# One encoder layer on one core: mixed tokens stored by token tile, pinned splits of the paired projections, and conditioning, combination and gate sums moved to other steps

## The chip, the cores and the metric

The kernel runs on one core of one Trainium2 chip. Time is device microseconds of one execution; the time before is the median of three runs. A profiled execution has a time of its own and a span, which runs from the first to the last recorded instruction. The engines are named as the profile names them: PE (TensorE, with PEld for its weight loads), DVE (VectorE), ACT (ScalarE), POOL (GpSimd) and SP (SyncE, which here only issues DMAs).

## The reference

One layer of an encoder for 1024 tokens of width 1024, float32 throughout:

```
mod = silu(c) @ w_ada + b_ada                      # sh1, sc1, gt1, sh2, sc2, gt2
h = rms_norm(x, g1) * (1 + sc1) + sh1
qa, ka, va, qb, kb, vb, gates = split(h @ w_in)
o_a = neighbourhood_attention(rms_norm(qa), rms_norm(ka), va, rpb)       # 8 heads on a 16 x 64 grid
for g, (window, dilation) in enumerate(((128, 1), (512, 4), (2048, 16))): # 4 heads each, partial rotary
    outs[g], lses[g] = dilated_window_attention(qb, kb, vb, window, dilation)
o_b = sum_g softmax_g(lses)[g] * outs[g]
merged = sigmoid(gate_a) * (o_a @ w_proj_a) + sigmoid(gate_b) * (o_b @ w_proj_b)
x = x + gt1 * (merged @ w_o)
h2 = rms_norm(x, g2) * (1 + sc2) + sh2
x = x + gt2 * ((silu(a) * up) @ w_ffn_out),  a, up = split(h2 @ w_ffn_in)
```

## The kernel before, in words

**Precision.** Every large product is made of three matrix multiplications. An operand is split into a high part (`whi`, ACT, a copy into the type fp32r) and a low part (`wlo`, the operand minus its high part, on DVE or POOL); `wsplit` does this. PE then adds high by high, high by low and low by high in PSUM (`PASS`).

**Fewer products.** Some of the large products are made by a seven-product scheme for 2 x 2 blocks: sums and differences of the operands' blocks are formed, seven block products replace eight. The token side of these sums ("mixed tokens") is made once, by `t_piece` in steps 9 to 26, and is written in high and low parts to the DRAM tensor `t_d`. There are four mixed blocks, named by `TD`: x1, w22, x3, x2, each 512 tokens (four tiles of 128) by 512 features (four slices of 128).

**The middle part of the kernel** is a loop over steps n = 6 to 91. In each step PE gets a few chunks of projection work from a list, `stream`, and one round of attention of an earlier unit (scores, transposes, product with v). Units are column groups of the projection: units 1 to 3 one at a time, units 4 to 9 as three pairs (`pair_units`). A pair has the products p1, p2, x1, x2, x4, x3, w22, each of four token tiles by four chunks. For a product, `when(s - 28 + 4*k, load)` loads weight slice k, `mix` forms the weight sum on POOL (tile `chain` or in place in `raw`), and `split` makes its high and low parts; `sload` loads one token tile of the mixed tokens (`smix`, high and low) from `t_d`. Pairs begin at about steps 28, 44 and 60; from step 58 on (`PAIRED`) attention runs in every step.

**What else is in these steps.** `ada_step` works on the conditioning: 64 small steps, each one multiply-add on DVE over a 128 x 512 piece of `w_ada` (tile `wa`, acc at L328 and L330), with one 512 KB load for two steps. `w1_combos` forms sums of the feed-forward weights on POOL for two column groups and writes them to `w1_d` (`w1m` loads, L881 to L887, stores at L889). `combine_prep` and `combine_step` combine the three dilated groups, in twelve pieces: DVE spreads the softmax weights over a tile `fb` (L720), PE transposes it (L729), DVE multiplies with the attention output `ut` that has been loaded from `u_d`, and adds into `oacc` (L737, L739, L740). From step 74 on `gate_prep` prepares the gate weights of column pairs (sums at L794, L796, L801, then `wsplit`), and from step 76 on `gate_pre` puts their products into the steps (L806), which read the tokens in `hT` as moving operand. For the phase "x1" that operand is the mixed block, reloaded from `t_d` into `hT` by `mixed_load`.

**What sets the order.** PE's instructions run in the order of the program. On ACT, DVE, POOL and SP a planner orders instructions by priority and readiness; those handed to `pin` keep the order of the program among themselves. Each engine then works through its queue strictly in order: an instruction that waits holds what is queued behind it, and a DMA that waits on SP holds all later loads. Tiles come from rings of buffers: `big` has 8, `raw` 6, the rings `hi` and `lo` 10 each.

Of the kernel before, what the change touches and what calls it, by code (L numbers as in the profile page):

```python
# [10 lines left out]
F32 = mybir.dt.float32  # L11
# [12 lines left out]
NRAW, NHL = 6, 10  # L24
# [5 lines left out]
GPHASE = ("w11", "w12", "x1", "x4")  # L30
GPREP = {74: (0, 0), 77: (0, 1), 82: (1, 0), 84: (1, 1), 86: (2, 0), 88: (2, 1), 90: (3, 0)}
GLOAD = {81: 1, 85: 2, 89: 3}
W1MIX = 36
MC11 = {0: (5, 6, 7, 2), 1: (0, 1)}
MKEEP = {3: 3, 4: 4, 5: 5, 6: 6, 7: 7}
MSLOT = {4: 2, 5: 0, 6: 1}
# [2 lines left out]
PP, QT, AQ, AT, AV = 100, 0, 0, 0, 0  # L39
EDGE, CFILL, AFILL, OFILL = 480, 64, 384, 32  # L40
WARM = 40
PAIRED, RBT, COMB = 58, 7, 68
XSQ = "avavaaaa"
XSC = "ddddvvvv"
XE = ("av", "vv", "aa", "aa", "vv", "aa", "va", "va")
# [3 lines left out]
def hybrid_layer(ctx: ExitStack, tc: tile.TileContext, x, colp, wada1, wada2, bada2, wqkv, wg, wpa, wpb,  # L49
# [17 lines left out]
    v_d = tc.dram_tile([8, S, 128], F32, name="v_d")  # L67
    sig_d = tc.dram_tile([KT, 5, 128, 512], F32, name="sig_d")
    h_d = tc.dram_tile([8, 128, S], F32, name="h_d")
    t_d = tc.dram_tile([2, 4, 128, 4, 512], F32, name="t_d")  # L70
    ga_d = tc.dram_tile([7, HT, 128, 512], F32, name="ga_d")
    x2_d = tc.dram_tile([S, D], F32, name="x2_d")
    w1_d = tc.dram_tile([2, 4, 128, 512], F32, name="w1_d")
# [41 lines left out]
    def fview(ap):  # L115
        return ap.bitcast(F32)
# [5 lines left out]
            tc.keep_in_program_order(d)  # L122
        return raw[:, :n]

    def wsplit(r, eng=None):
        n = r.shape[1]
        hi = wp.tile([128, 512], F32R, tag="hi", bufs=NHL, name="whi")
        lo = wp.tile([128, 512], F32R, tag="lo", bufs=NHL, name="wlo")
        nc.scalar.activation(hi[:, :n], r, AF.Copy)  # L129
        (eng or nc.gpsimd).tensor_sub(lo[:, :n], r, fview(hi[:, :n]))  # L130
        return hi, lo

# [568 lines left out]
    def combine_prep(i):  # L701
        pr, g, hf = i // 6, (i % 6) // 2, i % 2
        if g == 0 and hf == 0:
            cb["acc"] = big("oacc")
        ut = wp.tile([128, 512], F32, tag="raw", bufs=NRAW, name="ut")
        u = u_d[g * 2 + pr]
        if g == 0:
            pin(nc.sync.dma_start(ut, u[:, hf * 512:hf * 512 + 512]))
            uv = ut
        elif g == 1:  # L710
            pin(nc.sync.dma_start(ut.rearrange("p (r i) -> p r i", r=4),
                                  u.rearrange("p (r h i) -> p h r i", r=4, h=2)[:, hf]))
            uv = ut.rearrange("p (r i) -> p i r", r=4)
        else:
            pin(nc.sync.dma_start(ut.rearrange("p (t i) -> p t i", t=8),
                                  u.rearrange("p (t i) -> p t i", t=8)[:, :, hf * 64:hf * 64 + 64]))
            uv = ut.rearrange("p (t i) -> p i t", t=8)
        fb = ap_.tile([128, 4, 2, 64], F32, tag=("bm", "rtab")[i % 2], bufs=1, name="fb")
        for hd in range(2):
            nc.vector.tensor_copy(fb[:, :, hd, :], cb["fe"][:, g, hf * 4:hf * 4 + 4, pr, hd, None]  # L720
                                  .to_broadcast([128, 4, 64]))
        cb[i] = (fb, ut, uv, cb["acc"])
# [37 lines left out]

    def mixed_load(nm):
        for q in range(2):
            pin(nc.sync.dma_start(fview(hblk(*TBLK[nm])[q]), t_d[q, TD[nm]]))

    def gate_raw(i, q):
        return wload(wg[i, :, 4 * q:4 * q + 4, :], 512, True)
# [8 lines left out]
    def gate_prep(p, part):  # L775
        pr = GPAIRS[p]
        if part == 0:
            for i in pr if p == 0 else ():
                for q in (0, 1):
                    graw[i, q] = gate_raw(i, q)  # L780
            for nm, q in (("w11", 0), ("w12", 1)):
                for i in pr:
                    gwt[i, nm] = wsplit(graw[i, q])
            return
        if p == 0:
            z = big("wgx")
            for i in pr:
                for q in (2, 3):
                    graw[i, q] = gate_raw(i, q) if i == pr[0] else z[:, 512 * q - 1024:512 * q - 512]
            for q in (2, 3):  # L790
                pin(nc.sync.dma_start(graw[pr[1], q], wg[pr[1], :, 4 * q:4 * q + 4, :]))
        for i in pr:
            r = [graw.pop((i, q)) for q in range(4)]
            nc.vector.tensor_add(r[2], r[2], r[3])  # L794
            gwt[i, "x1"] = wsplit(r[2])
            nc.vector.tensor_sub(r[2], r[2], r[0])  # L796
            if p < 3:
                nc.sync.dma_start(sig_d[i, 4], r[2])
            else:
                glate[i] = r[2], r[3]  # L800
            nc.vector.tensor_sub(r[1], r[1], r[2])  # L801
            gwt[i, "x4"] = wsplit(r[1], nc.vector)

    def gate_mm(pb, w, b, k):
        for q, (x, y) in enumerate(PASS):
# [10 lines left out]
    def gate_pre(n):  # L816

        p, ph = divmod(n, 4)
        nm = GPHASE[ph]

        def chunk(c):
            j, k = divmod(c, 4)
            i = GPAIRS[p][j]
            if k == 0:
                gbank[i] = bank("d")
            gate_mm(gbank[i], gwt[i, nm], hblk(*TBLK[nm]), k)
            if k < 3:
                return
            if ph == 0:
                gacc[i] = [None, ap_.tile([128, 512], F32, tag=("bm", "rtab")[j], bufs=1, name="ga")]  # L830
            elif j == 0:
                z = big("gc")
                for jj in range(2):
                    g = gacc[GPAIRS[p][jj]]
                    g[len(g) if ph > 1 else 0:len(g) + 1 if ph > 1 else 1] = [z[:, 512 * jj:512 * jj + 512]]
            if ph == 0:
                nc.scalar.activation(gacc[i][1], gbank[i], AF.Copy)  # L837
            else:
                gate_open_out(i, nm, gbank[i])
            m = (1, 0, 2, 3)[ph]  # L840
            nc.sync.dma_start(sig_d[i, m], gacc[i][m])

        return [lambda c=c: chunk(c) for c in range(8)]
# [4 lines left out]
    def t_piece(m, part):  # L848
# [15 lines left out]
        else:  # L864
            for a in (0, 2):
                pin(nc.vector.tensor_sub(lo[:, a:a + 2], y[:, a:a + 2], fview(hi[:, a:a + 2])))
            for q, z in enumerate((hi, lo)):
                pin(nc.sync.dma_start(t_d[q, :, :, kk, 256 * pc:256 * pc + 256].rearrange("s p c -> p s c"), fview(z)))

    w1c = {}  # L870

# [226 lines left out]
    def pair_units(ua):  # L1098
        ub = ua + 1
        chain, ch = [], {}  # L1100
        for nm in PROD:
# [3 lines left out]
            for k in range(4):  # L1105
# [16 lines left out]
                        pin(nc.gpsimd.tensor_sub(ch[k], r[k], ch[k]))  # L1122

                def split(k=k, nm=nm, r=r, w=w):
                    w[k] = wsplit(ch[k] if nm in ("x1", "x2", "x3") else r[k], nc.vector if k % 2 else None)

                when(s - 28 + 4 * k, load)
                when(s - 12 + 2 * k, mix)
# [1 line left out]
            for t in range(4):  # L1130
                sm = {}
                if nm in TD:
                    def sload(t=t, nm=nm, sm=sm):
                        for q, tag in enumerate(("hi", "lo")):
                            z = wp.tile([128, 512], F32R, tag=tag, bufs=NHL, name="smix")
                            pin(nc.sync.dma_start(fview(z).rearrange("p (k q) -> p k q", k=4),
                                                  t_d[q, TD[nm], :, :, 128 * t:128 * t + 128]))
                            sm[q] = z

                    when(s + 4 * t - 10, sload)  # L1140
# [33 lines left out]
    for n in range(6, 92):  # L1174
# [82 lines left out]
                    at_turn(I, 1)  # L1257
        while chunks:
            chunk()
        for _ in range(0 if n < 8 else 2 if 28 <= n < PAIRED and n % 2 == 0 else 1):  # L1260
            if ada_state["i"] < 67:
                ada_step()
        for m in range(8):
# [4 lines left out]
                hT[q][0, 1] = quarter(q, 0, 1)  # L1268
            mixed_load("x1")
        for j in range(2):  # L1270
            if 0 <= n - W1MIX - 4 * j < 5:
                w1_combos(j, n - W1MIX - 4 * j)
        if n in GPREP:
            gate_prep(*GPREP[n])
        if n in GLOAD:
# [11 lines left out]
        elif 6 <= u < 10 and t == RBT:  # L1287
            bias_tabs(units[u])

    fill(ap_, AFILL, "afill")  # L1290

    ap_.release()
# [29 lines left out]
    def gate_prod(i, nm):  # L1322
        p = gate_bank()
        for k in range(4):
            gate_mm(p, gwt[i, nm], hblk(*TBLK[nm]), k)
        return p

    def room(n, shape, name, dtype=F32):
# [598 lines left out]
```

## Time and profile before

| | us |
|---|---|
| median of 3 runs | 1535.08 (1532.36 to 1535.8) |
| profiled execution, its own time | 1534.09 |
| its span | 1532.3 |
| PE busy | 1470.1 |
| DVE busy | 1118.4 |
| ACT busy | 715.4 |
| POOL busy | 668.0 |
| mean granted TensorE clock | 0.983 |

Read it by stages. Up to about 200 us the kernel loads, normalises and projects units 0 to 3; from about 200 to 540 us it works on the three pairs; from about 540 to 640 us come the last attention steps and the first gate products; after that the rest of the gates, the merge, the output projection and the feed-forward part. A row of a timeline gives start, duration, engine, line, operation and tiles; what stands in square brackets is the idle time of the engine just before it and what ended that idle time. The granted clock (PEclk) is a share of TensorE's full speed.

### The profile page before, as it was taken

How to read it: one execution, taken by the hardware profiler on the slowest of the kernel's cores; microseconds unless marked ns; L12 is line 12 of the kernel's file. 1: busy time of each engine (PE TensorE's matmuls, PEld its weight loads, DVE VectorE, ACT ScalarE, POOL GpSimd, SP SyncE). 2: the span in 40 equal slices, each digit the busy share in tenths (PEclk: the TensorE clock that was granted, in tenths of full speed). 3: DMA queues.
4: the chain of work that ended last, by engine and by line, in shares of the span. 5: the costliest groups of instructions: out<-in, count | busy, mean ns of one | idle time of the engine just before them, and what ended most of it. 6: DMA issues, size and time to landing. Idle time of an engine off the chain costs nothing. (4 is left out here: it accounts for less than half of the span.)

```text
span 1532.3 us, 24444 instructions
## 1 busy us (share of the span) xinstructions
PE 1470.1 (96%) x8024; PEld 1246.5 (81%) x8024; DVE 1118.4 (73%) x2210; ACT 715.4 (47%) x1807; POOL 668.0 (44%) x640
## 2 busy tenths in 40 slices
PE   8999989779899889999999999999999999999998
PEld 7999978668788767788888888888888888887886
DVE  6787767857888965468584488778867777599468
ACT  5657654544677756446442254222323233343442
POOL 0454344664133102345451120577777776104464
PEclk9999999888999999999999999999999999999999
DMA  9646577679656665494444135345433334798352
GB/s 365 239 156 224 173 247 240 203 246 306 197 169 205 182 192 209 155 359 143 129 135 168 69 110 165 112 157 164 166 132 107 107 104 146 259 375 278 98 153 101
DMA packets 211439, 285.16 MB, mean 186 GB/s; under 512 B 29136, under 2 KB 128112, under 8 KB 209520
## 3 DMA queue, kind: packets, MB, share of 16 engines
q1 hardware_dynamic: 192736, 269.96, 53.3%
q10 hardware_dynamic: 18576, 13.64, 2.7%
q8 instruction: 64, 1.05, 0.3%
q14 instruction: 63, 0.52, 0.1%
HBM read 218.67 MB, written 64.86 MB: 185 GB/s over the span
## 5 line engine op out<-in xcount | busy, mean ns | idle before, releaser
L129 ACT ACTIVATE whi<-raw 128x512 fp32r<-128x512 f32 (+2 forms) x313 | 182.6, 594 | 224.1 <-PE ps_t L1762 33.9
L130 POOL TENSOR_TENSOR wlo<-raw,whi 128x512 fp32r<-128x512 f32 (+2 forms) x116 | 153.1, 1327 | 207.0 <-ACT whi L129 151.2
L130 DVE TENSOR_TENSOR wlo<-raw,whi 128x512 fp32r<-128x512 f32 (+1 forms) x197 | 174.7, 900 | 61.5 <-ACT whi L129 57.3
L1151 PE MATMUL ps_d<-whi,smix 128*128 128x384 f32 x384 | 112.5, 359 | 15.0 <-DMA smix<-t_d 8.2
L341 PE MATMUL ps_d<-whi,hT 128*128 128x384 f32 x384 | 101.0, 338 | 0.0
L1151 PE MATMUL ps_d<-whi,hT 128*128 128x384 f32 x288 | 84.0, 354 | 16.4 <-DVE vs L397 9.7
L1542 POOL TENSOR_TENSOR e<-e,c 128x512 f32<-128x512 f32 x44 | 68.8, 1565 | 61.6 <-DVE c L1672 37.4
L129 ACT ACTIVATE whi<-ws 128x512 fp32r<-128x512 f32 x60 | 37.7, 628 | 119.4 <-DVE ws L1609 83.5
L1151 PEld LDWEIGHTS ps_d<-whi,smix 128*128 128x128 f32 x384 | 74.3, 199 | 18.1 <-issue 7.6
L806 PE MATMUL ps_d<-hT,whi 128*128 128x512 f32 x256 | 82.1, 402 | 1.8 <-ACT ga L837 1.8
L130 POOL TENSOR_TENSOR wlo<-m,whi 128x512 fp32r<-128x512 f32 x35 | 51.9, 1492 | 55.5 <-ACT whi L129 55.5
L1151 PE MATMUL ps_d<-wlo,smix 128*128 128x384 f32 x192 | 67.7, 353 | 5.3 <-POOL wlo L130 3.6
L384 POOL TENSOR_TENSOR ra<-qn,rtab 128x64 f32<-128x64 f32 x48 | 22.0, 459 | 115.2 <-DVE qn L375 64.9
L130 POOL TENSOR_TENSOR wlo<-gl,whi 128x512 fp32r<-128x512 f32 x26 | 35.9, 1394 | 82.4 <-ACT whi L129 82.4
L1151 PEld LDWEIGHTS ps_d<-whi,hT 128*128 128x128 f32 x288 | 54.4, 194 | 20.1 <-issue 12.2
L341 PEld LDWEIGHTS ps_d<-whi,hT 128*128 128x128 f32 x384 | 69.6, 188 | 0.5 <-issue 0.4
L1540 ACT ACTIVATE e<-e 128x512 f32<-128x512 f32 x44 | 27.4, 630 | 86.2 <-DVE e L1675 60.3
L341 PE MATMUL ps_d<-wlo,hT 128*128 128x384 f32 x192 | 64.2, 334 | 0.0
L1592 PE MATMUL ps_v<-h2T,whi 128*128 128x512 f32 x192 | 59.2, 389 | 0.0
L1592 PE MATMUL ps_s<-h2T,whi 128*128 128x512 f32 x192 | 59.1, 389 | 0.0
L609 ACT ACTIVATE P<-P,st 128x256 f32<-128x256 f32 (+2 forms) x100 | 45.6, 458 | 24.2 <-DVE st L607 24.2
L1592 PE MATMUL ps_d<-h2T,whi 128*128 128x512 f32 x184 | 56.7, 390 | 0.0
(445 smaller groups left out, 4498.4 us busy)
## 6 DMA issues: line engine op xcount, KB each, us to landing
raw<-in_w_dram SPq DMA_DIRECT2D x139, 256.0 KB
smix<-t_d SPq DMA_DIRECT2D x96, 256.0 KB
raw<-in_wqkv_dram SPq DMA_DIRECT2D x116, 192.0 KB
ga_d<-e SPq DMA_DIRECT2D x77, 256.0 KB
raw<-ga_d SPq DMA_DIRECT2D x77, 256.0 KB
wa<-in_wada_dram SPq DMA_DIRECT2D x32, 512.0 KB
m<-in_w_dram SPq DMA_DIRECT2D x44, 256.0 KB
xt<-in_x_dram SPq DMA_DIRECT2D x16, 512.0 KB
```

The source lines that it names most:

```text
L129: nc.scalar.activation(hi[:, :n], r, AF.Copy)
L130: (eng or nc.gpsimd).tensor_sub(lo[:, :n], r, fview(hi[:, :n]))
L341: nc.tensor.matmul(pd[:, :384], tok(a, k, t), U.w[k][b][:, :384], start=(k == 0 and i == 0), stop=(k == KT - 1 and i == 2))
L384: nc.gpsimd.tensor_tensor(v4(ra), v4(qn[:, :, 0:16]), tv(0, 0, 16), op=ALU.mult)
L609: nc.scalar.activation(C.P[h][:nq, c], C.P[h][:nq, c], AF.Exp, scale=-1.0, bias=nm, accum_out=sm)
L806: nc.tensor.matmul(pb, w[x][:, k * 128:(k + 1) * 128], b[y][:, k], start=(k == 0 and q == 0), stop=(k == 3 and q == 2))
L1151: nc.tensor.matmul(pd[:, :384], lhs, w[k][b][:, :384], start=(k == 0 and i == 0), stop=(k == 3 and i == 2))
L1540: nc.scalar.activation(sg, a, AF.Sigmoid)
L1542: nc.gpsimd.tensor_mul(sg, sg, up)
L1592: nc.tensor.matmul(pb, w[p][:, k * 128:(k + 1) * 128], b[q][:, k], start=(k == 0 and i == 0), stop=(k == 3 and i == 2))
```

## The change

It has six parts.

1. `t_d` is laid out by token tile: `[part, block, tile, 128, 4, 128]` in place of `[part, block, 128, 4, 512]`. A `smix` load of a tile then reads 2 KB runs in place of four runs of 512 bytes. A store of a mixed piece becomes two DMAs with runs of 512 bytes in place of one with runs of 1 KB (32 stores in place of 16). `mixed_load` reads 2 KB runs in place of 8 KB runs, and the block lies in `hT` by tiles, so that a gate product of a mixed block (x1, x2, x3, w22) reads its moving operand as four runs of 128 columns (`gblk`).
2. In the pairs, the high-part copy on ACT is pinned (`keep=True`), and of the four slices of a product only k = 3 has its low part on DVE; before it was k = 1 and k = 3. So 21 low parts go to POOL.
3. Two conditioning steps stand in each even step from 10 to 26; before they stood in the even steps from 28 to 56.
4. The sums of the feed-forward weights start at steps 30 and 47; before at 36 and 40.
5. The gate sums of the first three column pairs, and the low part of their x4 block, are made on POOL in place of DVE (24 operations).
6. The combination starts at step 79 in place of 68, and its tile `fb` comes from the `raw` ring in place of the tiles `bm` and `rtab`. The last of its two stores stands behind the loop.

```diff
-W1MIX = 36
+W1MIX = (30, 47)
-PAIRED, RBT, COMB = 58, 7, 68
+PAIRED, RBT, COMB = 58, 7, 79
-    t_d = tc.dram_tile([2, 4, 128, 4, 512], F32, name="t_d")
+    t_d = tc.dram_tile([2, 4, 4, 128, 4, 128], F32, name="t_d")
-    def wsplit(r, eng=None):
+    def wsplit(r, eng=None, keep=False):
...
-        nc.scalar.activation(hi[:, :n], r, AF.Copy)
+        h = nc.scalar.activation(hi[:, :n], r, AF.Copy)
+        if keep:
+            pin(h)
...
-        fb = ap_.tile([128, 4, 2, 64], F32, tag=("bm", "rtab")[i % 2], bufs=1, name="fb")
+        fb = wp.tile([128, 4, 2, 64], F32, tag="raw", bufs=NRAW, name="fb")
...
     def mixed_load(nm):
         for q in range(2):
-            pin(nc.sync.dma_start(fview(hblk(*TBLK[nm])[q]), t_d[q, TD[nm]]))
+            z = fview(hblk(*TBLK[nm])[q]).rearrange("p a n -> p (a n)").rearrange("p (t x) -> p t x", t=4)
+            pin(nc.sync.dma_start(z, t_d[q, TD[nm]].rearrange("t p k c -> p t (k c)")))
+
+    def gblk(nm):
+        z = hblk(*TBLK[nm])
+        if nm in TD:
+            z = [y.rearrange("p a n -> p (a n)").rearrange("p (t k c) -> p k t c", t=4, k=4) for y in z]
+        return z
...
+        eng = nc.vector if p == 3 else nc.gpsimd
         for i in pr:
             r = [graw.pop((i, q)) for q in range(4)]
-            nc.vector.tensor_add(r[2], r[2], r[3])
+            eng.tensor_add(r[2], r[2], r[3])
             gwt[i, "x1"] = wsplit(r[2])
-            nc.vector.tensor_sub(r[2], r[2], r[0])
+            eng.tensor_sub(r[2], r[2], r[0])
...
-            nc.vector.tensor_sub(r[1], r[1], r[2])
-            gwt[i, "x4"] = wsplit(r[1], nc.vector)
+            eng.tensor_sub(r[1], r[1], r[2])
+            gwt[i, "x4"] = wsplit(r[1], eng)
...
-                pin(nc.sync.dma_start(t_d[q, :, :, kk, 256 * pc:256 * pc + 256].rearrange("s p c -> p s c"), fview(z)))
+                for j in range(2):
+                    pin(nc.sync.dma_start(t_d[q, :, 2 * pc + j, :, kk].rearrange("s p c -> p s c"),
+                                          fview(z)[:, :, 128 * j:128 * j + 128]))
...
-                    w[k] = wsplit(ch[k] if nm in ("x1", "x2", "x3") else r[k], nc.vector if k % 2 else None)
+                    w[k] = wsplit(ch[k] if nm in ("x1", "x2", "x3") else r[k], nc.vector if k == 3 else None, True)
...
-                            pin(nc.sync.dma_start(fview(z).rearrange("p (k q) -> p k q", k=4),
-                                                  t_d[q, TD[nm], :, :, 128 * t:128 * t + 128]))
+                            pin(nc.sync.dma_start(fview(z).rearrange("p (k q) -> p k q", k=4), t_d[q, TD[nm], t]))
...
-        for _ in range(0 if n < 8 else 2 if 28 <= n < PAIRED and n % 2 == 0 else 1):
+        for _ in range(0 if n < 8 else 2 if 10 <= n < 28 and n % 2 == 0 else 1):
             if ada_state["i"] < 67:
                 ada_step()
...
-            if 0 <= n - W1MIX - 4 * j < 5:
-                w1_combos(j, n - W1MIX - 4 * j)
+            if 0 <= n - W1MIX[j] < 5:
+                w1_combos(j, n - W1MIX[j])
...
+    pin(nc.sync.dma_start(*cb.pop("out")))
     fill(ap_, AFILL, "afill")
```

The change moves instructions on the engines. Three places show it, each row a line of the program with the operation and its tiles. In the changed program line numbers are higher by 2 at L130, by 10 at L794 and by 12 from L877 to L1151.

The first is SP, which issues the loads, towards the end of the first pair. `w1m` and `w_d` belong to the feed-forward weight sums, `smix` are mixed tokens, `raw` weights of the pair, `v` values of an attention unit. Before:

```order
L1136 DMA smix<-t_d 128x4x128 x2
L120 DMA raw<-in_wqkv_dram 128x384
L1136 DMA smix<-t_d 128x4x128 x2
L889 DMA w_d<-w1m 128x512 x3
L877 DMA w1m<-in_w_dram 128x512 x4
L415 DMA v<-v_d 128x1024
L120 DMA raw<-in_wqkv_dram 128x384
L1136 DMA smix<-t_d 128x4x128 x2
```

Now:

```order
L1148 DMA smix<-t_d 128x512 x4
L120 DMA raw<-in_wqkv_dram 128x384
L1148 DMA smix<-t_d 128x512 x2
L417 DMA v<-v_d 128x1024
L120 DMA raw<-in_wqkv_dram 128x384
L1148 DMA smix<-t_d 128x512 x2
L120 DMA raw<-in_wqkv_dram 128x384
L299 DMA mod_d<-brow 4x128
```

Three stores and four loads of the weight sums no longer stand between two pairs of `smix` loads.

The second is POOL at the product x3 of the first pair. `chain` is a weight sum, `wlo` a low part, `ra`, `rb` and `qn` are the rotary embedding, which waits for DVE. Before:

```order
L1122 TENSOR_TENSOR chain<-raw,chain 128x384 x2
L130 TENSOR_TENSOR wlo<-chain,whi 128x384
L881 TENSOR_TENSOR w1m<-w1m 128x512
L1122 TENSOR_TENSOR chain<-raw,chain 128x384
L384 TENSOR_TENSOR ra<-qn,rtab 128x64
L385 TENSOR_TENSOR rb<-qn,rtab 128x4x8
L386 TENSOR_TENSOR rb<-qn,rtab 128x4x8
L387 TENSOR_TENSOR qn<-ra,rb 128x4x16
L1122 TENSOR_TENSOR chain<-raw,chain 128x384
```

Now:

```order
L1134 TENSOR_TENSOR chain<-raw,chain 128x384 x2
L132 TENSOR_TENSOR wlo<-chain,whi 128x384
L1134 TENSOR_TENSOR chain<-raw,chain 128x384
L132 TENSOR_TENSOR wlo<-chain,whi 128x384
L386 TENSOR_TENSOR ra<-qn,rtab 128x64
L387 TENSOR_TENSOR rb<-qn,rtab 128x4x8
L388 TENSOR_TENSOR rb<-qn,rtab 128x4x8
L386 TENSOR_TENSOR ra<-qn,rtab 128x64
L387 TENSOR_TENSOR rb<-qn,rtab 128x4x8
L388 TENSOR_TENSOR rb<-qn,rtab 128x4x8
L389 TENSOR_TENSOR qn<-ra,rb 128x4x16
L1134 TENSOR_TENSOR chain<-raw,chain 128x384
```

A second low part stands where a feed-forward sum stood, and the last weight sum still stands behind rotary work.

The third is DVE at the first gate sums. `raw` and `wgx` are gate weights, `fb` the spread weights of the combination, `qk` and `PT` operands that PE needs for attention, `gc` a gate sum that frees a PSUM bank. Before:

```order
L794 TENSOR_TENSOR raw<-raw 128x512
L547 RECIPROCAL sx<-sx 128x1
L720 COPY fb<-fe 128x4x64 x2
L456 SCALAR_TENSOR_TENSOR qk<-ps_v,hg,qk 128x2x64
L560 COPY PT<-ps_t 128x384
L457 TENSOR_TENSOR qk<-ps_v,qk 128x2x64
L547 RECIPROCAL sx<-sx 128x1
L814 TENSOR_TENSOR gc<-ga,ps_d 128x512
L794 TENSOR_TENSOR wgx<-wgx 128x512
L720 COPY fb<-fe 128x4x64 x2
L796 TENSOR_TENSOR raw<-raw 128x512
L801 TENSOR_TENSOR raw<-raw 128x512
```

Now:

```order
L824 TENSOR_TENSOR gc<-ga,ps_d 128x512
L722 COPY fb<-fe 128x4x64 x2
L546 ISA P,sx<-ps_s,rb 128x384
L546 ISA sx 128x1
L546 ISA P,sx<-ps_s,rb 128x384
L546 ISA sx 128x1
L549 RECIPROCAL sx<-sx 128x1
L562 COPY PT<-ps_t 128x384
L722 COPY fb<-fe 128x4x64 x2
L549 RECIPROCAL sx<-sx 128x1
L458 SCALAR_TENSOR_TENSOR qk<-ps_v,hg,qk 128x2x64
L459 TENSOR_TENSOR qk<-ps_v,qk 128x2x64
```

The gate sums have left DVE's queue, and the first `fb` copies stand beside the last steps of attention and the first gate products.

More of the change, by code (lines that the diff above doesn't have):

```diff
@@ L825, in chunk @@
                 gbank[i] = bank("d")
-            gate_mm(gbank[i], gwt[i, nm], hblk(*TBLK[nm]), k)
+            gate_mm(gbank[i], gwt[i, nm], gblk(nm), k)
             if k < 3:
@@ L1324, in gate_prod @@
         for k in range(4):
-            gate_mm(p, gwt[i, nm], hblk(*TBLK[nm]), k)
+            gate_mm(p, gwt[i, nm], gblk(nm), k)
         return p
```

## The prediction

> **What bounds the kernel now.** I read the span and busy times first, then the windows by stage, then PE's own timeline. (Columns of the windows: stretch, width, busy time of PE, PEld, DVE, ACT, POOL with instructions, granted clock, DMA share, GB/s.)
>
> ```profile
> span 1532.3 us, 24444 instructions
> PE 1470.1 (96%) x8024; PEld 1246.5 (81%) x8024; DVE 1118.4 (73%) x2210; ACT 715.4 (47%) x1807; POOL 668.0 (44%) x640
> 75.00:200.00 125.00, 125.00 (x898) 118.37 (x897) 98.67 (x278) 79.51 (x277) 56.43 (x113) 1.00 0.61 198
> 200.00:300.00 100.00, 85.65 (x601) 76.59 (x600) 71.99 (x204) 51.43 (x173) 48.90 (x79) 0.91 0.71 220
> 300.00:400.00 100.00, 81.14 (x551) 73.94 (x549) 69.48 (x206) 47.00 (x163) 44.26 (x54) 0.86 0.80 253
> 400.00:500.00 100.00, 95.40 (x697) 84.21 (x696) 83.08 (x279) 74.99 (x236) 30.59 (x30) 1.00 0.66 197
> 500.00:580.00 80.00, 67.28 (x461) 52.94 (x458) 65.09 (x194) 50.33 (x156) 9.23 (x8) 0.96 0.59 179
> 580.00:650.00 70.00, 69.81 (x423) 54.44 (x422) 32.27 (x85) 38.93 (x97) 20.95 (x17) 1.00 0.54 193
> 650.00:1375.00 725.00, 725.00 (x3233) 601.00 (x3232) 533.40 (x695) 269.42 (x482) 363.64 (x252) 1.00 0.48 162
> ```
>
> PE is the bound: it is full from 75 to 200 and again from 580 to 1375. Between 200 and 580 it stands idle for 14.35 + 18.86 + 4.60 + 12.72 = 50.5 us, and its granted clock is below 1 there. If the clock is either whole or half, the time at half clock is 2 x (0.09 x 100 + 0.14 x 100 + 0.04 x 80) = 52 us. A busy microsecond of it loses half of itself and an idle one nothing, so the loss lies between 0 and 26 us; I take the middle, 13. All that an edit of loads, splits and sums can win is then about 63 us, before 580 us. These waits make up much of it (in brackets the idle time just ahead of the row, and what ended it):
>
> ```profile
> 228.05 0.44 PE L1151 MATMUL ps_d<-wlo,smix 128*128 128x384 f32 x1 [1.65 <-DVE wlo L130]
> 277.38 0.69 PE L1151 MATMUL ps_d<-whi,smix 128*128 128x384 f32 x1 [4.82 <-ACT whi L129]
> 279.72 0.69 PE L1151 MATMUL ps_d<-wlo,smix 128*128 128x384 f32 x1 [1.66 <-POOL wlo L130]
> 309.97 0.66 PE L1151 MATMUL ps_d<-whi,smix 128*128 128x384 f32 x1 [6.93 <-DMA smix<-t_d]
> 345.40 0.66 PE L1151 MATMUL ps_d<-whi,hT 128*128 128x384 f32 x1 [4.62 <-DVE vs L397]
> 391.29 0.66 PE L1151 MATMUL ps_d<-whi,hT 128*128 128x384 f32 x1 [3.15 <-DVE vs L397]
> 510.72 0.66 PE L729 MATMUL ps_t<-ident,fb 128*128 128x128 f32 x4 [1.70 <-DVE PT L560]
> 561.36 1.08 PE L729 MATMUL ps_t<-ident,fb 128*128 128x128 f32 x4 [2.31 <-DVE fb L720]
> 312.00:314.00 2.00, 2.00 (x8) 2.00 (x7) 1.60 (x2) 1.05 (x2) 2.00 (x3) 0.50 1.04 406
> ```
>
> No one engine is late throughout: a low part, a load, an eviction and a combination tile take turns. Behind the 6.93 us wait PE runs at half clock as late as 314, so a long wait costs more than its length.
>
> **The change part by part.** *The weight sums leave SP's path.* SP's timeline (start, duration, line) shows what stood ahead of the late smix load:
>
> ```profile
> 291.19 1.19 SPq L1136 DMA_DIRECT2D smix<-t_d  x2
> 297.25 2.85 SPq L889 DMA_DIRECT2D w_d<-w1m  x3
> 304.54 1.32 SPq L1136 DMA_DIRECT2D smix<-t_d  x2
> 314.62 10.30 SPq L315 DMA_DIRECT2D brow<-in_bada_dram  x2
> 336.27 7.49 SPq L669 DMA_DIRECT2D stat_d<-st  x8
> ```
>
> From 292.4 SP issues nothing until three stores of a weight sum go at 297.25; loads follow in a burst, and the next smix pair goes at 304.54, 12 us after the one before ended. In the changed order these stores and loads stand elsewhere. I take back the whole 6.93: 7 (bounds 0, if another wait lies right behind, and 7). The sums come back in steps 30 to 34 and 47 to 51, the second set ahead of pair 2's weight chains, in the stretch with 4.60 us of idle time. There the stores can hold SP as at 297; that would cost 0 to 7, and I take 3.
>
> *Low parts and the weight chain of x3.*
>
> ```profile
> 271.32 1.59 POOL L881 TENSOR_TENSOR w1m<-w1m 128x512 f32<-128x512 f32 x1
> 275.78 0.98 POOL L1122 TENSOR_TENSOR chain<-raw,chain 128x384 f32<-128x384 f32 x1
> L130 POOL TENSOR_TENSOR wlo<-chain,whi x18: 985/1020/1535, 223.7 to 480.6; 128x384 fp32r<-128x384 f32 x18
> L130 DVE TENSOR_TENSOR wlo<-chain,whi x18: 544/558/1322, 227.4 to 491.7; 128x384 fp32r<-128x384 f32 x18
> ```
>
> (The three numbers are the shortest, the median and the longest, in ns.) The wait of 4.82 at 277.38 ends with ACT's copy of a chain sum that POOL made from 275.78 on. Ahead of it the 1.59 us sum goes, one low part of 1.02 comes, and the rotary work stays, so this alone wins 0.6; pinned copies, which no later work can overtake, and the freed DVE (21 x 0.56 = 12 us) win some of the rest. The three waits at 228, 277 and 280 are 8.1 us together: I take 3, bounds 0 and 8. POOL gets 21 x 1.02 = 21 us in stages where it is busy 49, 44 and 31 of 100 us; its capacity covers that, its order is a rival below.
>
> *Conditioning earlier.*
>
> ```profile
> L330 DVE SCALAR_TENSOR_TENSOR acc<-wa,cact,acc x56: 732/743/1497, 77.8 to 392.6; 128x512 f32<-128x512 f32 x56
> 75.00:200.00 125.00, 14.82 (x19) 1.00 0.61 198
> 200.00:420.00 220.00, 29.23 (x37) 0.90 0.76 236
> 383.86 1.52 DVE L330 SCALAR_TENSOR_TENSOR acc<-wa,cact,acc 128x512 f32<-128x512 f32 x2
> ```
>
> (The middle rows are windows of L330 alone: 19 of the 56 before 200, 37 after.) By the end of step 27 the changed program has 29 of all 64 conditioning steps behind it, the old one 20. So nine steps, 9 x 0.743 = 6.7 us of DVE and 4.5 loads of 512 KB, move ahead of 200 us. DVE is busy 98.67 of 125 there and PE never waits: 26 us of free DVE time hide them; without that cover they would cost 6.7. The later steps come singly and no longer in pairs of 1.5 us, like the one at 383.86 a little ahead of the wait at 391.29. Beside the 6.93 and the 4.62, 7.3 us of waits are left in 300 to 400, and 4.60 in 400 to 500. Of these 11.9 I take a third, 4; bounds 0 and 12.
>
> *The second hold on SP*, 10.30 us for `brow` at 314.62, ends in a burst; 7.49 us of statistics stores follow, and the 4.62 us wait at 345.40. In the changed order `brow` stands behind two more pairs of smix loads, but the stores remain: I take 3, bounds 0 and 4.6.
>
> *Gate sums and combination.*
>
> ```profile
> L720 DVE COPY fb<-fe x24: 274/286/309, 431.5 to 563.7; 128x256 f32<-128x256 f32 x24
> L739 DVE TENSOR_TENSOR ps_t<-ut,ps_t x8: 1024/1060/1112, 503.8 to 574.5; 128x512 f32<-128x512 f32 x8
> L740 DVE TENSOR_TENSOR oacc<-oacc,ps_t 128x512 f32<-128x512 f32 x8 | 5.5, 686 | 0.1
> L794 DVE TENSOR_TENSOR gl<-gl x6: 691/692/695, 586.2 to 644.9; 128x512 f32<-128x512 f32 x6
>   DMA gl<-in_wg_dram: 11.9, 6
> 555.20 1.07 DVE L739 TENSOR_TENSOR ps_t<-ut,ps_t 128x512 f32<-128x512 f32 x1 [3.87 <-DMA ut<-u_d]
> ```
>
> A piece costs DVE 2 x 0.286 + 1.06 + 0.69 = 2.3 us, all twelve at most 28. They leave the stage 500 to 580, where DVE is busy 65.09 of 80 and owes PE the `PT` and `fb` tiles, for the one with 32.27 of 70, where PE waits 0.19. The 24 gate operations leave DVE as well, 24 x 0.69 = 17 us, and with six of them its 11.9 us of waiting for `gl`. POOL gets 24 x 1.59 = 38 us by the row of L881, where it is busy 9.23 of 80 and 20.95 of 70. Of the 12.72 us of this stage I take half, 6; bounds 0 and 12.7. With `ut` loads late, as the 3.87 at 555.20, some of it would come back behind 580.
>
> *Layout.*
>
> ```profile
> L1136 SPq DMA_DIRECT2D smix<-t_d x96: 517/574/1762, 202.4 to 511.7; - x96
> L868 SPq DMA_DIRECT2D t_d<-tp x16: 359/377/951, 92.6 to 191.9; - x16
> L806 PE MATMUL ps_v<-hT,whi 128*128 128x512 f32 x64 | 19.7, 389 | 0.0
> ```
>
> Sixteen more stores are 16 x 0.38 = 6 us of SP between 75 and 200, hidden by a PE that waits for nothing there. The 96 smix loads move the same bytes in longer runs; an issue takes 0.57 us. I count nothing beside the terms above. The gate products of the four mixed blocks, 4 blocks x 8 columns x 12 = 384, now read four runs of 128 columns. The nearest rows are 0.389 us for one run of 512, and four products of 128 columns in 0.66 at 510.72. So the extra lies between 0 and 384 x 0.27 = 104 us; as the columns are the same and the number of instructions too, I take 0.
>
> The waits won are 7 + 3 + 4 + 3 + 6 = 23 of the 50.5; the clock gives its share, 13 x 23/50.5 = 6. New costs are the 3 above and 2 for POOL in DVE's way (0 to 34, below). Together 23 + 6 - 5 = 24. The profiled execution took 1534.1 (its span and 1.8); 1534.1 - 24 = 1510.1, and the median stands 1.0 above that execution: **1511**.
>
> **The rivals.** *Nearly the whole pool goes*: if the bursts on SP feed most waits, 200 to 580 would run as 400 to 500 does, with 0.046 x 380 = 17 us of idle time. That wins 33, and 13 x 33/50.5 = 8 of clock: 41, so 1494. For it speaks the DMA share of 0.80 in the worst window; against it that the brackets name four releasers.
>
> *The waits move on.* Where one wait goes, the next part is late: behind the 4.82 at 277.38 comes 1.66 two microseconds later. Only the 7 and 2 of clock are kept, less the 3 for the second sums: 6, so 1529. Against it: 400 to 500 holds the same work with fewer conditioning steps and no weight sums, and idles only 4.60.
>
> *No change*, 1535: an end that waits for something else. Against it: PE is full after 580, so nothing there takes a gain back.
>
> *Slower: POOL delivers last.* With three of four low parts behind rotary work in POOL's queue, PE waits in each of the 21 products as at 279.72, 1.6 us: 34 in all, in place of the 2 counted above: 24 + 2 - 34 = -8, so 1543. It decides from 26/21 = 1.2 us a product. For it: a part takes 1.02 on POOL and 0.56 on DVE. The longest L330 (1.50) and the longest low part on DVE (1.32) are twice their usual, so something holds DVE at times. Against it: a product lasts 380/21 = 18 us, its three parts take 3, and POOL idles half the time. The Trainium skill, "SBUF — State Buffer", section "Who interferes with whom", says that a DVE instruction with two inputs in SBUF and a GpSimd instruction reading SBUF shut each other out for the whole instruction. By that rule the 45 operations moved could hold DVE for up to 21 + 38 = 59 us, twice the 29 that they free; the doubled longest rows agree, the medians, close to the shortest, say that it is rare here.
>
> *Slower: the four runs.* If each costs as a product of its own, 104 us: 1615. It decides from 24/384 = 0.06 us a product. No row of the profile has such an operand, so nothing there speaks for it; the equal number of columns speaks against it.
>
> **How the numbers follow.** The forecast, a gain of 12 to 36, gets 0.56; the whole pool 0.15; waits that move on 0.14; no change 0.05; POOL last 0.07; the four runs 0.03. A change within 0.2% (3 us) is about what a measurement of this kernel cannot tell from none. Faster: 0.56 + 0.15 + 0.12 of the moved waits = 0.83; same: 0.02 of these + 0.05 = 0.07; slower: 0.07 + 0.03 = 0.10. The range reaches from 1488, 6 beyond the whole pool, to 1533, behind the moved waits; outside it lie no change, both slower cases and the tails, under 2 in 10.
>
> **What would show it.** Right: no wait of over 3 us for smix at the end of pair 1; a clock above 0.95 in 300 to 400; idle PE in 200 to 500 near 22 us, not 38; waits for fb and PT gone before 580, and the gate stage still full. Wrong: POOL's `wlo` ahead of most products with a microsecond or more (POOL last); products of mixed blocks above 0.45 us (four runs); waits of the same length for other parts (waits move on); `ut` or `fb` as releaser behind 580.

## The result and the profile after

The changed kernel takes 1544.33 us (median of 6 runs, 1540.36 to 1547.6); the kernel before, timed in the same rounds and before them, 1533.72 (6 runs, 1528.79 to 1536.47). The ratio is 1.0068, with a 95% interval of 1.0045 to 1.0092: the change made the kernel slower by some 10 us. The forecast was 1511 and its range ended at 1533.

The page of the changed kernel and its windows by stage (columns as before):

```profile
span 1545.8 us, 24460 instructions
PE 1482.9 (96%) x8024; PEld 1253.9 (81%) x8024; DVE 1114.9 (72%) x2165; ACT 713.1 (46%) x1807; POOL 713.9 (46%) x685
200.00:300.00 100.00, 80.33 (x526) 69.99 (x525) 60.85 (x175) 46.14 (x154) 50.22 (x81) 0.90 0.65 203
300.00:400.00 100.00, 85.13 (x578) 76.34 (x578) 70.56 (x206) 49.88 (x178) 49.80 (x65) 0.90 0.71 228
400.00:500.00 100.00, 87.30 (x560) 74.73 (x559) 73.88 (x220) 58.98 (x188) 31.39 (x30) 0.90 0.58 180
500.00:580.00 80.00, 76.58 (x542) 62.71 (x541) 60.59 (x204) 61.97 (x198) 27.04 (x24) 0.98 0.54 177
```

In two stages there is less idle time of PE than before: 14.87 us in place of 18.86 in 300 to 400, and 3.42 in place of 12.72 in 500 to 580. (The changed kernel runs up to 19 us late there, so one window does not hold quite the same work in both.) What came instead stands in 200 to 300 (19.67 for 14.35) and above all in 400 to 500 (12.70 for 4.60, and a granted clock of 0.90 for 1.00).

Over 200 to 580 PE is idle for 50.7 us, as long as before. So the loss is not in standing still: the spans differ by 13.5 us, and PE's busy time by 12.8 (1482.9 for 1470.1). The clock makes most of this. Counted from the trace's clock records, PE is busy at half clock for 56.0 us of this stretch with the change and for 37.9 before; half of the difference, 9 us, is lost. (A product of 384 columns with `wlo` and `smix` takes 0.334 us in the median and up to 0.689.)

The times at which the first gate product and the first product after the last attention step start tell where it is lost. (The group of line 806 before, 816 after: shortest, median and longest in ns, first and last start; the second row of each pair is the one behind attention.) Before, and then after:

```profile
L806 PE MATMUL ps_d<-hT,whi x256: 387/389/774, 533.0 to 728.8; 128*128 128x512 f32 x128
L806 PE MATMUL ps_v<-hT,whi x64: 389/389/389, 647.7 to 726.1; 128*128 128x512 f32 x64
```

```profile
L816 PE MATMUL ps_d<-hT,whi x256: 387/390/505, 552.3 to 743.1; 128*128 128x512 f32 x128
L816 PE MATMUL ps_v<-hT,whi x64: 388/389/482, 661.9 to 740.4; 128*128 128x512 f32 x64
```

Up to the first gate product the changed kernel loses 19.3 us; from there to the end of attention it wins 5.1 (109.6 for 114.7); behind that the two run alike.

Who ended PE's waits in 200 to 580 (total, number of waits, longest). Before:

```profile
PE ps_d L1151 <- DVE vs L397: 9.7, 4, 4.6
PE ps_d L1151 <- DMA smix<-t_d: 8.2, 2, 6.9
PE ps_d L1151 <- ACT whi L129: 6.1, 3, 4.8
PE ps_d L1151 <- POOL wlo L130: 3.6, 3, 1.7
PE ps_d L1151 <- DVE wlo L130: 1.7, 1, 1.7
```

After:

```profile
PE ps_d L1162 <- ACT whi L129: 19.4, 10, 4.4
PE ps_d L1162 <- POOL wlo L132: 12.4, 17, 1.3
PE ps_d L1162 <- DVE wlo L132: 5.9, 5, 2.5
```

The waits for `vs` and for `smix` are gone, as forecast; one of 4.6 us for another result of DVE, the sum `hT` at L1104, has come. Waits for a weight's high or low part have grown from 11.4 us in 7 places to 37.7 in 32. A high part and its low part are links of one chain, and the wait at 437.34 shows it from its end to its start (timelines of PE, POOL, ACT and DVE of the changed kernel; in brackets the idle time ahead):

```profile
437.34 0.47 PE L1162 MATMUL ps_d<-whi,hT 128*128 128x384 f32 x1 [3.69 <-ACT whi L129]
437.36 1.96 POOL L132 TENSOR_TENSOR wlo<-raw,whi 128x384 fp32r<-128x384 f32 x2 [14.88 <-ACT whi L129]
436.78 0.92 ACT L129 ACTIVATE whi<-raw 128x384 fp32r<-128x384 f32 x2
435.77 0.20 ACT L371 ACTIVATE rv<-rv 128x4 f32<-128x4 f32 x1 [2.65 <-DVE rz L374]
434.88 0.29 DVE L399 TENSOR_TENSOR vs<-hT,ps_d 128x128 f32<-128x128 f32 x1 [2.21 <-DMA v_d<-vs]
```

PE waits for a high part. ACT makes it at 436.78, right behind steps of a unit's normalisation (`rv`) that waited for DVE, which itself waited for a buffer whose store was under way. POOL, whose next instruction is the low part, had stood idle for 14.88 us. ACT starts the copy without a wait for the weights: what held it was its place in the queue. In ACT's queue, in the kernel as changed (place in the queue, counted over ACT's activations and DMA issues; line, operation, tiles with their numbers):

```
751 L550 ACTIVATE P_6068<-P_6068,sx_6069 128x256
752 L372 ACTIVATE ry_6032<-rv_6031 128x4
753 L129 ACTIVATE whi_6047<-raw_5758 128x384
754 L129 ACTIVATE whi_6085<-raw_5846 128x384
755 L370 ACTIVATE rv_6101<-ss4_6099,eps_98 128x4
```

and with the two copies free to be ordered:

```
721 L364 ACTIVATE sq_5879<-qn_5874 128x256
722 L402 DMA v_d_76<-vs_5876 16x8x128
723 L129 ACTIVATE whi_6047<-raw_5758 128x384
724 L129 ACTIVATE whi_6085<-raw_5846 128x384
725 L456 ACTIVATE qk_5419<-ps_v_5949,hg_87 128x4x64
```

The pin has put the same two copies 30 places later, behind a softmax and a normalisation. In the traces of the two kernels, 70 of the 84 copies in the pairs stand later with the pin, none earlier; over all 84 it is 16.0 places on average and 56 at most. Among themselves the copies stand in the same order with the pin and without.

### The profile page after: what moved, and what is told of

The parts are those of the page before. It is cut to its first block, busy times and chain, and to the rows that moved or that the text cites. A ratio compares the mean times of both kernels' runs of the same rounds, so it can differ in the third digit from the quotient of the medians.

```text
span 1545.8 us, 24460 instructions
## 1 busy us (share of the span) xinstructions
PE 1482.9 (96%) x8024; PEld 1253.9 (81%) x8024; DVE 1114.9 (72%) x2165; ACT 713.1 (46%) x1807; POOL 713.9 (46%) x685
## 5 line engine op out<-in xcount | busy, mean ns | idle before, releaser
L132 POOL TENSOR_TENSOR wlo<-raw,whi 128x512 fp32r<-128x512 f32 (+2 forms) x130 | 167.2, 1295 | 208.1 <-ACT whi L129 196.8
L132 DVE TENSOR_TENSOR wlo<-raw,whi 128x512 fp32r<-128x512 f32 (+1 forms) x183 | 160.5, 892 | 52.9 <-ACT whi L129 48.8
L129 ACT ACTIVATE whi<-ws 128x512 fp32r<-128x512 f32 x60 | 37.7, 628 | 118.9 <-DVE ws L1621 77.4
L1162 PE MATMUL ps_d<-wlo,smix 128*128 128x384 f32 x192 | 71.4, 372 | 14.1 <-POOL wlo L132 8.6
L332 DVE SCALAR_TENSOR_TENSOR acc<-wa,cact,acc 128x512 f32<-128x512 f32 x56 | 51.5, 920 | 9.0 <-DMA wa<-in_wada_dram 8.9
L132 POOL TENSOR_TENSOR wlo<-chain,whi 128x384 fp32r<-128x384 f32 x27 | 28.0, 1046 | 64.3 <-ACT whi L129 53.7
```

What stands on the lines that cost most here:

```text
L129: h = nc.scalar.activation(hi[:, :n], r, AF.Copy)
L332: nc.vector.scalar_tensor_tensor(ada_acc[c], wa, cact[:, kk:kk + 1], ada_acc[c], op0=ALU.mult, op1=ALU.add)
L1162: nc.tensor.matmul(pd[:, :384], lhs, w[k][b][:, :384], start=(k == 0 and i == 0), stop=(k == 3 and i == 2))
```

## The experiments

Three theories: P, the pinned copies on ACT come too late; Q, POOL's low parts come too late; R, another part makes everything late. Each kernel was timed in five rounds beside the kernel before, and ratios below are to that kernel; 0.001 is 1.5 us. The pinned kernel has 1.0068.

**Part 2 undone.**

```diff
-  w[k] = wsplit(..., nc.vector if k == 3 else None, True)
+  w[k] = wsplit(..., nc.vector if k % 2 else None)
```

> The changed kernel (1544.3) with part 2 undone: copies of the pairs' high parts free to be ordered, low parts of slices 1 and 3 on DVE again. Theory P (the pinned copies on ACT come too late, behind attention's work in ACT's queue): the 19.4 us of waits for ACT's whi and most of the 12.4 for POOL's wlo go, the time falls by 20 to 30 us, to 1515 to 1525. Theory Q (POOL's low parts come too late): about the same fall. Theory R (another part of the change makes everything late, and the weight parts are only the place where it shows): less than 5 us, about 1540.

1506.10 us, ratio 0.9852 (0.9830 to 0.9874). Without this one line the rest of the change wins 22.7 us. R falls.

**The pin alone taken away**, low parts of slices 0 to 2 still on POOL.

```diff
-  w[k] = wsplit(..., nc.vector if k == 3 else None, True)
+  w[k] = wsplit(..., nc.vector if k == 3 else None)
```

> The changed kernel with the copies unpinned alone; low parts of slices 0, 1 and 2 stay on POOL. Theory P: as fast as with all of part 2 undone, within 4 us, and waits for ACT's whi under 8 us in 200 to 580. Theory Q: falls by less than 5 us, POOL's wlo stays a releaser for 10 us or more. Theory R: no change.

1505.64 us, ratio 0.9842 (0.9822 to 0.9863): 24.2 us faster than before. The difference to the pinned kernel, 0.0226, is 35 us (39 by the medians, but the kernel before was at 1533.7 beside the one and at 1530.0 beside the other). Span and busy times, windows, PE's waits in 200 to 580, and the gate products:

```profile
span 1500.9 us, 24456 instructions
PE 1458.9 (97%) x8024; PEld 1239.3 (83%) x8024; DVE 1100.8 (73%) x2165; ACT 712.1 (47%) x1807; POOL 714.3 (48%) x685
200.00:300.00 100.00, 85.86 (x598) 77.20 (x597) 68.11 (x200) 53.46 (x177) 54.56 (x89) 0.93 0.70 230
300.00:400.00 100.00, 89.66 (x657) 81.81 (x656) 78.03 (x232) 57.21 (x200) 54.51 (x64) 0.98 0.81 259
400.00:500.00 100.00, 95.82 (x697) 84.51 (x696) 81.27 (x281) 75.84 (x249) 35.47 (x34) 0.98 0.59 193
500.00:580.00 80.00, 77.73 (x529) 60.01 (x528) 53.29 (x164) 56.40 (x163) 38.53 (x30) 1.00 0.63 212
PE ps_d L1162 <- ACT whi L129: 5.3, 2, 2.8
PE ps_d L1162 <- POOL wlo L132: 1.4, 3, 0.6
L816 PE MATMUL ps_d<-hT,whi x256: 387/389/505, 509.2 to 699.2; 128*128 128x512 f32 x128
L816 PE MATMUL ps_v<-hT,whi x64: 388/389/481, 617.9 to 696.4; 128*128 128x512 f32 x64
```

Waits for POOL's `wlo` fall from 12.4 us to 1.4 although POOL makes as many low parts as before: they were late because the copies were, and Q falls. The first gate product starts at 509.2, 24 us ahead of the kernel before.

The two profiled executions, with the pin and without, differ by 44.9 us, more than the medians do. 24.0 of these are longer busy time of PE (1482.9 for 1458.9), most of it from the clock: PE is busy at half clock for 56.0 us of 200 to 580 with the pin and for 19.7 without. The other 20.9 are idle time.

The pin's price is that of the whole order that the planner makes with it. In the traces, 74 instructions on ACT stand more than ten places away from where they stand without the pin, but also 47 on DVE and 9 on POOL, and none on SP. No run moved the copies on ACT alone.

**Pinned, with slices 1 and 3 on DVE.**

```diff
-  w[k] = wsplit(..., nc.vector if k == 3 else None, True)
+  w[k] = wsplit(..., nc.vector if k % 2 else None, True)
```

> The changed kernel with the copies pinned as they are, and the low parts of slices 1 and 3 on DVE as before. Theory P: no change or at most 5 us faster, waits for whi stay near 19 us. Theory Q: falls by 15 us or more, waits for POOL's wlo go. Theory R: no change.

1552.06 us, ratio 1.0150 (1.0123 to 1.0177). POOL gets its 21 low parts back off its hands, and the kernel is slower still: by 12.6 us in the ratios, 7.7 in the medians. Q would have had it faster, and none of the theories had said that it would be slower.

```profile
PE ps_d L1162 <- ACT whi L129: 14.1, 10, 3.1
PE ps_d L1162 <- DVE wlo L132: 11.4, 9, 2.6
PE ps_d L1162 <- POOL wlo L132: 8.6, 14, 2.0
PE ps_d L1162 <- issue: 7.1, 2, 5.5
```

The waits go over from POOL's low parts to DVE's (5.9 us for these with three parts on POOL), but all waits for weight parts come to 34.1 us, less than the 37.7 above. What is more is 7.1 us of idle time that the view puts down to no wait ("issue"), and the two profiled executions differ by 2.3 us only. What makes this kernel slower stays open. Without the pin the place of the low parts makes no difference that can be measured (0.9852 and 0.9842).

**The kernel before with part 2 alone** (the copies' `pin` and the new rule for k put into it).

> The kernel before (1533.7) with part 2 alone. Theories P and Q: slower by 15 to 35 us, waits for whi and wlo of 25 us or more in 200 to 580. Theory R: within 5 us of the kernel before.

1558.62 us, ratio 1.0192 (1.0175 to 1.0209): slower by 29 us, with these waits in 200 to 580:

```profile
PE ps_d L1153 <- POOL wlo L132: 18.3, 22, 2.5
PE ps_d L1153 <- ACT whi L129: 18.1, 13, 5.8
```

So part 2 costs nearly as much in the old kernel as the pin does in the changed one (35). This run does not part the pin from the low parts on POOL; it shows that the cost needs none of the other five parts of the change. P stands.

**Pinned, but split three chunks earlier in the program.**

```diff
-  when(s - 7 + 2 * k, split)
+  when(s - 10 + 2 * k, split)
```

> The changed kernel with its copies still pinned, but the split written three chunks earlier in the program (at s - 10 + 2k in place of s - 7 + 2k), right after the weight sums. If what costs is the place that a pin freezes (one step too late), most of the 39 us between pinned and unpinned comes back: 1515 or less. If any fixed order costs, since a copy then waits behind whatever attention work the program writes ahead of it, less than half comes back: 1525 or more.

1535.78 us, ratio 1.0011 (0.9997 to 1.0026): 8.7 us of the 35 come back, a quarter. In ACT's queue the copies still stand 13.0 places later than in the unpinned kernel, where it was 16.0. At this place in the program, too, the pin is dear: without it, the same edit gives 0.9861 (next run), 23 us less. So the pin costs at both places that were tried; other places were not.

**Unpinned, split three chunks earlier** (the same edit, without the pin).

> The unpinned kernel with the split written three chunks earlier, as in the pinned run before (where it won 9 of 39 us). Without the pin the order on ACT goes by readiness, so the place in the program should hardly count: within 3 us of the unpinned kernel. If copies are still late without the pin (5.3 us of waits for whi are left in 200 to 580): faster by 3 to 6 us.

1511.77 us, ratio 0.9861 (0.9840 to 0.9882): nothing won; the interval overlaps that of the unpinned kernel, and the middle is 3 us above. Its waits for `whi` fall to 3.5 us, those for low parts rise to 8.5.

The other runs take the unpinned kernel (0.9842) and undo one more part.

**Conditioning back.**

```diff
-  2 if 10 <= n < 28 and n % 2 == 0 else 1
+  2 if 28 <= n < PAIRED and n % 2 == 0 else 1
```

> The unpinned kernel (1505.6) with the conditioning steps back in the even steps 28 to 56. The prediction's term: slower by 4 to 6 us. If conditioning carries most of the gain of 24: slower by 12 or more. If the one-by-one steps hold DVE on their loads: faster.

1513.77 us, ratio 0.9883 (0.9864 to 0.9903): 6.3 us slower. The waits for DVE's `vs` return (2.6 us in the unpinned kernel), and those for POOL's low parts grow (1.4 there):

```profile
PE ps_d L1162 <- POOL wlo L132: 7.0, 6, 2.2
PE ps_d L1162 <- DVE vs L399: 6.6, 3, 4.7
```

**Weight sums back.** `W1MIX = (36, 40)` in place of `(30, 47)`.

> The unpinned kernel with the feed-forward weight sums back at steps 36 and 40. The prediction's terms (7 won at the end of pair 1, 3 lost in pair 2, and a part of the 3 on POOL): slower by 4 to 8 us, with a wait of 3 us or more for smix near 300. If the shorter smix issues alone had freed SP: no change.

1520.23 us, ratio 0.9914 (0.9897 to 0.9931): 11 us slower. Timelines of PE and SP:

```profile
315.37 0.66 PE L1162 MATMUL ps_d<-whi,smix 128*128 128x384 f32 x1 [8.62 <-DMA smix<-t_d]
295.57 0.84 SPq L1148 DMA_DIRECT2D smix<-t_d  x2
296.46 9.54 SPq L901 DMA_DIRECT2D w_d<-w1m  x4
306.04 1.90 SPq L889 DMA_DIRECT2D w1m<-in_w_dram  x4
311.26 0.80 SPq L1148 DMA_DIRECT2D smix<-t_d  x2
```

The stores and loads of the weight sums stand between two pairs of `smix` again, and PE's long wait is back where it was before the change.

**Layout back**: `t_d`, its stores, its loads, `mixed_load` and the gate operand as before the change.

> The unpinned kernel with the mixed tokens stored by feature slice as before, so smix loads, stores, reloads and the gate products' operand are the old ones. The prediction's term is 0: within 3 us of the unpinned kernel. If the longer runs (smix issue 382 ns in place of 574) carry the gain: slower by 6 us or more. If the operand in four runs costs PE anything: faster.

1508.19 us, ratio 0.9836 (0.9816 to 0.9856): no difference. The smix issues are shorter in the new layout (382 ns for 574 in the median), but nothing waits for that, and the gate products' median of 389 ns is the same for either operand.

**Combination back at step 68**, `fb` still in the ring `raw`.

```diff
-PAIRED, RBT, COMB = 58, 7, 79
+PAIRED, RBT, COMB = 58, 7, 68
```

> The unpinned kernel (ratio 0.9842 to the kernel before) with the combination back at step 68; its tile fb stays in the raw ring and the gate sums stay on POOL. The prediction's term for combination and gate sums together was 6, and conditioning and weight sums measured 6 and 11 of the 24 us in all, so 5 to 8 are left: slower by 3 to 8 us if the combination carries them, within 3 us if the gate sums do.

1526.36 us, ratio 0.9953 (0.9935 to 0.9970): 17 us slower, far beyond the 8 expected. One wait of PE for `fb` is 8.5 us, and DVE's wait ahead of an `fb` copy was for POOL's gate sums in the same ring; so the mixture could have made the cost.

**Gate sums back on DVE** (`eng = nc.vector`).

> The unpinned kernel with the 24 gate operations back on DVE, the combination at step 79. If the gate sums carry part of the rest: slower by 3 to 8 us. If they only matter beside the combination: within 3 us.

1508.59 us, ratio 0.9841 (0.9820 to 0.9863): no difference.

**Both back.**

> The unpinned kernel with both the combination at step 68 and the gate sums on DVE. If the parts add up to the whole gain of 24: slower by 5 to 8 us. If less than 3, the rest of the gain belongs to something not undone so far (the fb ring, or parts that need each other).

1523.53 us, ratio 0.9936 (0.9917 to 0.9956): 14 us slower, again the combination.

**Combination and `fb` back**: step 68, and `fb` in the tiles `bm` and `rtab` as before the change.

> The unpinned kernel with the whole of part 6 undone: the combination at step 68 and its tile fb in the tiles bm and rtab again; gate sums stay on POOL. If the raw ring made the cost of the run before it (the 8.5 us wait for fb): the ratio falls from 0.9953 to about 0.990, 8 us above the unpinned kernel's 0.9842, near the prediction's 6. If the combination's place alone costs it: 0.994 to 0.997.

1526.88 us, ratio 0.9955 (0.9938 to 0.9971): as slow as with `fb` in the ring, so the ring does not show and the place of the combination does. Its windows:

```profile
400.00:500.00 100.00, 95.27 (x691) 84.04 (x689) 82.48 (x282) 74.63 (x240) 35.39 (x34) 0.97 0.63 205
500.00:580.00 80.00, 62.80 (x402) 46.83 (x400) 48.87 (x153) 42.74 (x130) 17.77 (x14) 0.89 0.47 158
```

Up to 500 it runs like the unpinned kernel; in 500 to 580 PE stands for 17.2 us in place of 2.3, and the clock falls to 0.89.

Undone one by one, conditioning, weight sums and combination cost 6 + 11 + 17 = 34 us, while all parts without the pin win 24. So they do not simply add up. Where the cause of the `smix` wait or of the idle time in 500 to 580 comes back alone, the wait is longer than in the kernel before (8.62 for 6.93; 17.2 for 12.72); the waits for `vs` are not (6.6 for 9.7). Which wait absorbs which was not taken apart.

## Why the prediction was wrong

**The step that failed** is in the part on low parts: "pinned copies, which no later work can overtake, and the freed DVE win some of the rest", counted as a gain within a term of 3, with bounds 0 and 8. It had no bound on the side of a loss. The runs show a loss of 35 us for the pin (1.0068 against 0.9842), 29 with the rest of part 2 in the kernel before. A pin holds a copy back as much as it holds others off: 70 of 84 copies stood later in ACT's queue. That could be read beforehand from the order of the instructions on ACT; the prediction showed the orders of SP, POOL and DVE and not that of ACT, the engine whose instructions are pinned.

**The rest of the sum** came out right as a whole: 24 us were forecast, and 24.2 measured once the pin is gone (0.0158 of 1533.7). The waits and the places named were mostly right, but that the total fits so closely is in part luck: several terms were missed by a factor of two or more, and their gains do not add up. Term by term:

- *Weight sums*, 7 less 3, 4 in all and a share of the clock: 11 when undone. The wait returned at the place named, between stores and loads on SP. The cost of 3 in pair 2 did not show, and its place was wrong: in the unpinned kernel the second set's stores go at 348.8 to 362.5, in the stage 300 to 400 and not in 400 to 500. PE's two waits there, 1.61 and 1.20 us, are for DVE and not for `smix`.
- *Conditioning*, 4 and a share of the clock: 6.3. The waits for `vs` that were named are 4.0 us longer with it, but those for POOL's `wlo`, which were not, 5.6.
- *Combination and gate sums*, 6: from the first gate product to the end of attention the changed kernel takes 5.1 us less, the unpinned one 6.0 (108.7 for 114.7). Undone alone, the combination costs 17, and the idle time in 500 to 580 alone is 14.9 longer (17.2 for 2.3), where the upper bound was 12.7; the gate sums cost nothing, so the 17 us of DVE that they freed, and its 11.9 us of waiting, had been hidden.
- *Layout*, 0: -1 us, within the interval; no loss from the four runs of columns, with 389 ns as before.
- *The second hold on SP*, 3: no run undid it alone; no wait for `vs` above 1.8 us is left in the unpinned kernel.
- *Low parts without the pin*, 3, and *POOL in DVE's way*, 2: neither shows; the runs with two and with three of four parts on POOL differ by 0.0010, within their intervals.
- *The waits won*, 23 of 50.5: 19.6 in the unpinned profile (14.14 + 10.34 + 4.18 + 2.27 = 30.9 left).
- *The clock*, 6: this term was too small. By the prediction's own way, 2 x (0.07 + 0.02 + 0.02) x 100 = 22 us at half clock are left where it was 52, and a quarter of that difference, 7.5, is won. The quarter came from taking the middle between a PE that is idle and one that is busy all through these stretches. Counted in the traces, PE is busy in 37.9 of 51.2 us at half clock before, and in 19.7 of 20.5 in the unpinned kernel. That is a loss of 19 us, not 13, and a gain of 9. With the 19.6 it makes 28.7 of the 31.4 us between these two profiled executions.

**The rival "POOL delivers last"** named 1543, and 1544 came, but not by its mechanism: with three of four low parts on POOL and no pin, POOL's `wlo` costs 1.4 us, and with two of them back on DVE the pinned kernel became slower. Its sign in the profile, POOL's `wlo` ahead of most products, did appear (17 waits), though only four of them reach a microsecond; the sign alone did not tell a slow engine from one that is served late. POOL's 14.88 us of idle time ahead of such a part does.

**What it would show.** No wait for smix at the end of pair 1, and waits for `fb` gone before 580: both seen. Waits for `PT` did not go: 4.6 us are left in 200 to 580 of 6.5. A clock above 0.95 in 300 to 400 and a full gate stage came only without the pin (0.98; 70.00 of 70, with it 68.73). The idle time in 200 to 500 was to be near 22 us and not 38: with the pin it is 47.2, without it 28.7, in between.

## What to carry to other kernels

Fixing an instruction's place in a queue is a change of order like any other: read what now stands ahead of it on its own engine, and give it a price on both sides. When a profile shows waits for a part that one engine makes, look first at that engine's idle time ahead of it; an engine that waits is not the cause. And undo the parts of a change one by one before judging them together: here one line cost 35 us and hid a gain of 24. Lastly, compare PE's busy time and not only its waits: of the 44.9 us between the profiled executions with the pin and without, 24.0 are longer busy time, most of it from the clock.

## What the runs showed of the hardware

A DVE multiply-add that starts while POOL is in a low part takes longer, in the rows below about twice as long; one that has already begun holds up POOL's part instead. In the changed kernel, conditioning steps on DVE, and POOL's work around them:

```profile
198.61 2.43 POOL L132 TENSOR_TENSOR wlo<-raw,whi 128x384 fp32r<-128x384 f32 x2
200.01 1.57 DVE L332 SCALAR_TENSOR_TENSOR acc<-wa,cact,acc 128x512 f32<-128x512 f32 x1
318.50 0.74 DVE L332 SCALAR_TENSOR_TENSOR acc<-wa,cact,acc 128x512 f32<-128x512 f32 x1
318.67 1.44 POOL L132 TENSOR_TENSOR wlo<-raw,whi 128x384 fp32r<-128x384 f32 x1 [6.86 <-ACT whi L129]
436.74 0.74 DVE L332 SCALAR_TENSOR_TENSOR acc<-wa,cact,acc 128x512 f32<-128x512 f32 x1
438.31 1.56 DVE L332 SCALAR_TENSOR_TENSOR acc<-wa,cact,acc 128x512 f32<-128x512 f32 x1
```

The step at 436.74 is nearly over when POOL ends its wait at 437.36, and takes 0.74 us. Those at 200.01 and 438.31 begin while POOL makes low parts (the row at 198.61, and the one at 437.36 shown above) and take 1.57 and 1.56. The step at 318.50 keeps its 0.74, and the part that POOL begins 0.17 us after it takes 1.44, where the low parts of weight sums before took 1.02 in the median. Of the 56 steps in the changed kernel 11 take over 1.2 us, and all 11 overlap work of POOL; 14 of those at 0.85 us or less overlap some too. In the unpinned kernel one long step (1.65 us at 389.63) overlaps none on record.

Over all 56 steps the mean is 0.787 us in the kernel before, 0.920 with the change and 0.941 in the unpinned kernel:

```profile
L330 DVE SCALAR_TENSOR_TENSOR acc<-wa,cact,acc 128x512 f32<-128x512 f32 x56 | 44.1, 787 | 4.7 <-DMA wa<-in_wada_dram 4.5
```

```profile
L332 DVE SCALAR_TENSOR_TENSOR acc<-wa,cact,acc 128x512 f32<-128x512 f32 x56 | 52.7, 941 | 9.2 <-DMA wa<-in_wada_dram 9.0
```

Where the steps stand counts for most of this: with the conditioning back in its old steps and the 45 operations still on POOL the mean is 0.825. So the prediction's "rare" was too little once the steps are moved, and its 0.743 a step, a median, was no mean. The Trainium skill, "SBUF — State Buffer", section "Who interferes with whom", says that such a DVE instruction and a GpSimd instruction that reads SBUF shut each other out; these rows agree with it. What it costs in time is small here: 21 low parts more on POOL changed nothing that could be measured (0.9852 and 0.9842).
